# Summing the first third of a modulation on VectorE, ScalarE and GpSimd in place of TensorE

## The chip, the cores and the metric

The kernel runs as one launch on one NeuronCore of a Trainium2 chip. The metric is the device time of one execution in microseconds (us). The engines are named as in the profile: PE (TensorE), DVE (VectorE), ACT (ScalarE), POOL (GpSimd) and SP (SyncE, which here only issues transfers).

## The reference

A layer of two blocks on 256 tokens of width 1024. The first is a feed-forward network (FFN), a mixer of three attentions, and a second FFN. The second block is steered by a modulation of two conditioning vectors: `c` for the 256 tokens, and `c_ctx` for 256 context tokens.

```python
def modulation(cvec, p):
    return jnp.split(jax.nn.silu(cvec) @ p['mod_w'] + p['mod_b'], 6, axis=-1)   # mod_w: [1024, 6 * 1024]
...
    h_ctx = rmsnorm(ctx, p['norm1_pre']) * (1.0 + m_ctx[1]) + m_ctx[0]          # context states
    h = rmsnorm(x, p['norm1_pre']) * (1.0 + m_lat[1]) + m_lat[0]                # tokens
    mixed, _ = token_mixer_2(h, p, ctx_states)
    x = x + m_lat[2] * rmsnorm(mixed, p['norm1_post'])
    h2 = rmsnorm(x, p['norm2_pre']) * (1.0 + m_lat[4]) + m_lat[3]
    x = x + m_lat[5] * rmsnorm(expert_choice_moe(h2, p), p['norm2_post'])       # 16 experts
```

The first third of the modulation, 2048 of its 6144 columns, is the shift and the scale of the first norm (`m[0]`, `m[1]`). It is needed for both vectors. The other two thirds are needed for `c` alone.

## The kernel before

All arrays are fp32. A dense product is made of three: each weight block of 128 rows by 1024 columns (or a regrouping of that size, 512 KB) is loaded by SP into `wraw` (four buffers), rounded by ACT to its high part `wh` (L245), and DVE subtracts that to get the low part `wl` (L246). Both parts have two buffers (`wsp`). PE then adds up high times high (L299), high weight times low input (L301) and low weight times high input (L302). In the FFN one such weight block feeds 24 products of 128x256. The text calls this a split. A new `wh` waits until PE is done with the block two before it. Four splits make one block of 256 hidden columns; then follow a tanh on ACT (L390) and two operations of DVE on PSUM (L391, L392), and every second 128 rows of hidden columns are split in turn (`fh`, `fl`).

`modulation(side, blocks, after)` (L789) is called twice: for block 0 ahead of the first FFN's blocks (`start`, L1856), and for blocks 1 and 2 in the second FFN. For each of 8 rows of 128 and two halves it loads 512 KB of `mod_w` into `mraw`, of which there are three buffers. These 16 loads a block are issued by POOL (L827).

- Block 0: four products a row and two a half, 64 in all, with `sc[:, k, :]` (32 columns, of which two are the vectors) as the stationary operand and 512 columns of `mraw` as the moving one (L831). They add up in one PSUM bank `px`, in four groups of 32 partitions.
- Blocks 1 and 2: row 0 is scaled by ACT into `acc` (L834), row 4 is multiplied and added by DVE (L836), and each of the other rows is scaled in place by ACT (L838) and added to `acc` by POOL (L839). Four products with a column of ones (L844) then sum over the partitions.

Afterwards DVE adds the bias (L846); for block 0 four transposes (L864) and small DVE operations bring the result feature-major into `mfm` (L871, L873). The context's norm (`norm_mod_T`, L879) uses it, and with it the context's recurrence (`context_states`, L1251), whose PE work lies between the blocks of the first FFN.

The order of instructions on each engine is fixed when the program is built. A planner simulates the program and lets each engine take the earliest ready instruction, those traced first ahead of others. `modulation` is traced ahead of the FFN's blocks. On the chip each engine works through its own list in order, and waits at semaphores.

Tiles of a pool that is closed give their memory to the next pool opened on the same side. The modulation's pool `md_t`, the pool of `bias_rows` (L414), and the context's pools `cx_t` and `cx_p` follow one another on the right side.

Of the kernel before, what the change touches and what calls it, by code (L numbers as in the profile page):

```python
# [18 lines left out]
T = 256  # L19
D = 1024  # L20
# [145 lines left out]
def _body(nc, tc, ctx, A, out):  # L166
# [42 lines left out]
    def rsqrt(ss, p, n, eps, op=ALU.add, pool=None):  # L209
        """1/sqrt(ss + eps) (or of max(ss, eps)) on [p, n]; ss may come in two parts to add."""  # L210
# [25 lines left out]
    def mean_sq_halves(x_ap, junk):  # L236
        """The mean square of a row in two parts, for rsqrt."""
        ss = small.tile([128, 2], F32, name="ssq")
        for nh in range(2):
            ns = slice(nh * 512, nh * 512 + 512)  # L240
            S.activation(junk[:, ns], x_ap[:, ns], AF.Square, scale=1.0 / 32, accum_out=ss[:, nh:nh + 1])
        return ss[:, 0:1], ss[:, 1:2]
# [5 lines left out]
    def transposes(dst_fn, src, n, dense=True):  # L248
        """PE-transpose n 128-column blocks of src; dst_fn(j0, k, ps) takes each bank's worth."""
# [8 lines left out]
    # this many of 1024 columns of a weight split have their low part from Pool  # L258
    share = [0]

    def wsplit(src, a, b, pool=None, name="w", eng=None, raw=None):
        """[a * 128, b] weights (a * b <= 1024) as a list of a (high, low) pairs of [128, b]."""
# [14 lines left out]
    def proj_tok(hT, w, kc, n0, n):  # L277
        """[128 tok, n] x 2 token tiles of h @ w[:, n0:n0+n]."""
# [13 lines left out]
    def proj_feat_acc(o, parts, hT, k0, bank0):  # L292
        """Accumulates feature-major products into o(c); the first to touch a bank starts it."""
# [11 lines left out]
    def proj_feat(hT, w, n0, n, take):  # L305
        """Feature-major [128 f, 256 tok] chunks of h @ w[:, n0:n0+n], n <= 512; take(c, ps)."""
# [14 lines left out]
    def norm_T(hT, t, x, xn, gain_bc):  # L321
        """rms norm of one token tile with a gain row, transposed and split in two parts into hT."""
# [6 lines left out]
    def in_turn(normed):  # L329
        """Both token tiles' norms ahead of what follows from the first."""  # L330
# [4 lines left out]
    def wide(w, nk, lhs, spare, done):  # L335
        """[T, D] of nk * 128 rows of w; the last rows' products go token tile by token tile, and
        done(t, two banks) follows each. lhs(k) gives the two parts [128, T]."""
# [27 lines left out]
    def ffn(xs, hT, gain, wg, wu, wd, hooks, then):  # L365
        """hooks: other work to issue before (-1) or after a block of hidden columns. hT is None where
        the norm is still to be done; then(pool, scratch) gives what follows for a finished token tile."""
# [43 lines left out]
    # ---------------------------------------------------------------- attention block  # L411
    skew = dram.tile([20, 128, 384], F32, name="skew")

    def bias_rows():  # L414
        """Bias by distance for every head (masked), once per partition, for a skewed load."""
# [14 lines left out]
    def attention(xs, hT, next_gain):  # L430
        """The block on the normed input hT; returns the normed input of the next, of gain next_gain."""
        with ExitStack() as fx:
# [55 lines left out]
            def evac_later(jobs, last=None):  # L488
                """(columns, take) projections, each block's take issued after the next block's products."""
# [7 lines left out]
            # ---- projections  # L497
# [65 lines left out]
            # ---- attention  # L563
            def softmax(lg, mx):
                """exp(lg - mx) in place; returns 1/sum."""
# [123 lines left out]
            def swept(attn):  # L689
                """Both query tiles, each head's output after the next one's logits."""  # L690
# [12 lines left out]
            def gates(i, nh):  # L703
                """1 + tanh of half the gate: twice its sigmoid."""
# [23 lines left out]
            def branch(w, kc, oT, nh, gs):  # L728
                """y += sigmoid(gate) * (o @ w), a factor 2 left in."""
# [55 lines left out]
    # ---------------------------------------------------------------- modulation  # L785
# [3 lines left out]
    def modulation(side, blocks, after=None):  # L789
        """Rows of silu(c) @ mod_w + mod_b; block 0 goes feature-major to mfm, the others to mrows, with  # L790
        the gains of the norms they meet (and a half) in them. For block 0 the
        tensor engine sums, for two vectors at once; the others are of one vector only, and their sums
        over a partition are Pool's. A generator: those start on each step, and end on the next."""
# [1103 lines left out]
```

## Time and profile before

| what | value |
|---|---|
| device time, median of 3 runs | 2231.14 us (2227.08 to 2231.18) |
| span of the profiled execution, first to last instruction | 2224.2 us |
| PE busy | 1826.4 us, 82% |
| DVE, ACT, POOL busy | 887.3, 589.9, 335.4 us |

The profile records one execution; it gives that execution's span, and no device time of its own beside it. The span lies 6.9 us under the median of the runs and 2.9 us under their lowest. Busy times are shares of the whole span, so they average over stages with different limits.

### The profile page before, as it was taken

What the parts mean: (1) busy time and instruction counts of PE and PEld (TensorE: products, weight loads), DVE (VectorE), ACT (ScalarE), POOL (GpSimd) and SP (SyncE); (2) the same over time, 40 slices, a digit from 0 to 9 for tenths busy, and PEclk for the clock granted to TensorE, in tenths of its full rate; (3) what the DMA queues carried; (4) which work ended last, traced back from release to release, by engine and by line L of the source; (5) the groups of instructions that cost most, each with busy time, mean ns of one, the idle gap of its engine ahead of it and who ended that gap; (6) DMA issues with size and microseconds to landing.
All of it is one profiled execution on the core that took longest, in us unless ns stands there. A gap on an engine that the chain in (4) does not pass through costs nothing.

```text
span 2224.2 us, 28420 instructions
## 1 busy us (share of the span) xinstructions
PE 1826.4 (82%) x11441; PEld 1108.2 (50%) x11442; DVE 887.3 (40%) x1611; ACT 589.9 (27%) x954; POOL 335.4 (15%) x332
## 2 busy tenths in 40 slices
PE   7999999999988899898999876766766666667775
PEld 5888877777768877888687521111111111111111
DVE  4577855865757765777647410000000000000001
ACT  3345443544436544453314200000000000000001
POOL 2111013210325540235233200000000000000000
PEclk9999989999989999989889887677677787777667
DMA  8654545444448855424336899999999999999997
GB/s 296 222 167 134 171 131 171 136 145 121 132 143 270 280 185 182 141 81 113 115 105 220 314 409 410 410 409 406 407 407 406 407 407 410 410 411 409 406 407 302
DMA packets 237046, 600.95 MB, mean 270 GB/s; under 512 B 35384, under 2 KB 91217, under 8 KB 204146
## 3 DMA queue, kind: packets, MB, share of 16 engines
q1 hardware_dynamic: 200464, 551.89, 67.6%
q0 software_dynamic: 10496, 36.08, 4.9%
q10 hardware_dynamic: 25954, 11.16, 1.9%
q8 instruction: 90, 1.47, 0.3%
q14 instruction: 42, 0.34, 0.0%
HBM read 593.25 MB, written 9.75 MB: 271 GB/s over the span
## 4 chain that ended last, share of the span: by engine, by line
DMA 42%; PE 41%; DVE 8%; ACT 3%; issue 3%; POOL 1%; SPq 0%; ACTq 0%; DVEq 0%; POOLq 0%
DMA ring<-exp_w 39%; PE mm L302 4%; PE mm L299 3%; PE mm L288 3%; PE mm L301 3%; PE mm L287 3%; PE mm L289 3%; DVE wl L246 2%; PE mm L346 2%; PE mm L345 2%; PE mm L349 2%; PE px L1779 1%; DMA wraw<-w_in 1%; ACT wh L245 1%; PE tr L1812 1%
## 5 line engine op out<-in xcount | busy, mean ns | idle before, releaser
L1779 PE MATMUL px<-ring,xeT 128*32 128x512 f32 x2048 | 370.0, 812 | 181.9 <-DMA ring<-exp_w 181.7
L246 DVE TENSOR_TENSOR wl<-wraw,wh 128x1024 fp32r<-128x1024 f32 (+2 forms) x243 | 317.5, 1307 | 174.2 <-ACT wh L245 169.9
L245 ACT ACTIVATE wh<-wraw 128x1024 fp32r<-128x1024 f32 (+2 forms) x243 | 254.5, 1048 | 352.5 <-PE mm L301 143.5
L1779 PEld LDWEIGHTS px<-ring,xeT 128*32 128x32 f32 x2048 | 48.7, 123 | 474.6 <-DMA ring<-exp_w 440.4
L302 PE MATMUL mm<-hh,wl 128*128 128x256 f32 x912 | 266.6, 294 | 18.6 <-DVE wl L246 16.6
L299 PE MATMUL mm<-hh,wh 128*128 128x256 f32 x912 | 265.7, 292 | 2.1 <-ACT hh L245 2.1
L301 PE MATMUL mm<-hl,wh 128*128 128x256 f32 x912 | 264.1, 290 | 1.7 <-DVE hl L246 1.6
L1791 DVE SCALAR_TENSOR_TENSOR mth<-mth,px 128x512 f32<-128x512 f32 x16 | 11.0, 687 | 580.4 <-ACT mth L1790 580.4
L1812 PE MATMUL tr<-ring,hid 128*32 128x512 f32 x1024 | 166.8, 758 | 77.8 <-DMA ring<-exp_w 65.1
L302 PEld LDWEIGHTS mm<-hh,wl 128*128 128x128 f32 x912 | 178.6, 196 | 33.2 <-DVE wl L246 21.4
L299 PEld LDWEIGHTS mm<-hh,wh 128*128 128x128 f32 x912 | 179.6, 197 | 11.4 <-issue 7.6
L301 PEld LDWEIGHTS mm<-hl,wh 128*128 128x128 f32 x912 | 179.5, 197 | 6.6 <-issue 3.9
L1815 ACT ACTIVATE ye<-tr 128x512 f32<-128x512 f32 x32 | 19.1, 597 | 566.7 <-PE tr L1812 566.7
L1625 POOL TENSOR_SCALAR rsz<-ss 128x1 f32<-128x1 f32 x2 | 0.6, 302 | 952.9 <-ACT ring L1625 952.8
L288 PE MATMUL mm<-wl,hh 128*128 128x512 f32 (+2 forms) x320 | 127.9, 400 | 2.3 <-DVE wl L246 2.0
L1812 PEld LDWEIGHTS tr<-ring,hid 128*32 128x32 f32 x1024 | 26.4, 124 | 203.4 <-DMA ring<-exp_w 143.8
L289 PE MATMUL mm<-wh,hl 128*128 128x512 f32 (+2 forms) x320 | 124.6, 390 | 0.0
L287 PE MATMUL mm<-wh,hh 128*128 128x512 f32 (+2 forms) x320 | 117.7, 400 | 6.7 <-DVE wi L525 3.6
L1817 PE MATMUL mm<-ye,pgT 128*128 128x512 f32 x128 | 92.8, 865 | 24.0 <-ACT ye L1815 24.0
L1792 DVE SCALAR_TENSOR_TENSOR mth<-mth,px 128x512 f32<-128x512 f32 x16 | 11.0, 687 | 253.0 <-PE px L1779 253.0
L1790 ACT ACTIVATE mth<-px 128x512 f32<-128x512 f32 x16 | 9.5, 597 | 283.5 <-PE px L1779 283.5
L1817 PEld LDWEIGHTS mm<-ye,pgT 128*128 128x128 f32 x128 | 30.1, 260 | 88.4 <-ACT ye L1815 63.7
(756 smaller groups left out, 2792.4 us busy)
## 6 DMA issues: line engine op xcount, KB each, us to landing
ring<-exp_w SPq DMA_DIRECT2D x384, 1024.0 KB
wraw<-w_in SPq DMA_DIRECT2D x107, 512.0 KB
mraw<-mod_w POOLq DMA_DIRECT2D x48, 512.0 KB, 5.1
wraw<-ffn_w_gate SPq DMA_DIRECT2D x44, 512.0 KB
wraw<-ffn_w_up SPq DMA_DIRECT2D x44, 512.0 KB
wraw<-ffn_w_down SPq DMA_DIRECT2D x44, 512.0 KB
wraw<-w_out SPq DMA_DIRECT2D x11, 512.0 KB
skew<-bd POOLq DMA_DIRECT2D x1, 3840.0 KB, 27.7
```

Of the source, the lines that this page charges most:

```text
L245: S.activation(dst_h, src, AF.Copy)
L246: (eng or V).tensor_tensor(dst_l, src, dst_h.bitcast(F32), op=ALU.subtract)
L287: PE.matmul(ps[t], hh[:, k, sl], wh, start=(k == 0), stop=False)
L288: PE.matmul(ps[t], hh[:, k, sl], wl, start=False, stop=False)
L289: PE.matmul(ps[t], hl[:, k, sl], wh, start=False, stop=(k == kc - 1))
L299: PE.matmul(o(c), wh[:, cs], hh[:, k, :], start=(k == 0 and bank0(c)), stop=False, skip_group_check=True)
L301: PE.matmul(o(c), wh[:, cs], hl[:, k, :], start=False, stop=False, skip_group_check=True)
L302: PE.matmul(o(c), wl[:, cs], hh[:, k, :], start=False, stop=(k == KC - 1), skip_group_check=True)
L345: PE.matmul(acc[t][nh], fh[:, sl], wh[:, ns], start=(k == 0), stop=False)
L1779: PE.matmul(ps[32 * g:32 * g + 32, :], xeT[:, k, es], wt[:, 0, g * 512:(g + 1) * 512], start=(k == 0), stop=(k == KC - 1), skip_group_chec ...
L1812: PE.matmul(pe2[32 * g:32 * g + 32, :], hid[:, q, 32 * g:32 * g + 32], w2t[:, g, :], start=(q == 0), stop=(q == 3), skip_group_check=True)
L1817: PE.matmul(acc[t][nh], pgT[:, t * 128:(t + 1) * 128], ye, start=(e == 0), stop=(e == NE - 1))
```

## The change

For block 0 the 64 products go. Every `mraw` is read by two engines: DVE multiplies it by the first vector's value and adds it to `acc`, and ACT multiplies it by the second vector's value into a new tile `part` (two buffers), which POOL adds to another sum `acc2`. For row 0 DVE and ACT write the sums directly. At the end two columns of ones bring both sums into one PSUM bank by eight products. `acc`, `acc2` and `part` are new tiles in `md_t` for block 0. Blocks 1 and 2 keep their operations.

```diff
-            one = tmp.tile([128, 32], F32, name="one")
-            V.memset(one, 0.0)
-            V.memset(one[:, 0:1], 1.0)
+            one = [tmp.tile([128, 32], F32, name=f"one{v}") for v in range(1 if blocks[0] else 2)]
+            for v, o in enumerate(one):
+                V.memset(o, 0.0)
+                V.memset(o[:, v:v + 1], 1.0)
...
-                if b:
-                    acc = tmp.tile([128, 2048], F32, name="acc")
-                else:
-                    ps = psX.tile([128, 512], F32, name="px")
+                acc = tmp.tile([128, 2048], F32, name="acc")
+                if b == 0:
+                    acc2 = tmp.tile([128, 2048], F32, name="acc2")
...
                         if b == 0:
-                            for gg in range(2):
-                                g = hf * 2 + gg
-                                PE.matmul(ps[32 * g:32 * g + 32, :], sc[:, k, :], raw[:, gg * 512:gg * 512 + 512],
-                                          start=(k == 0), stop=(k == KC - 1), skip_group_check=True)
+                            if k == 0:
+                                V.tensor_scalar(acc[:, hs], raw, sc[:, k, 0:1], None, op0=ALU.mult)
+                                S.activation(acc2[:, hs], raw, AF.Copy, scale=sc[:, k, 1:2])
+                            else:
+                                V.scalar_tensor_tensor(acc[:, hs], raw, sc[:, k, 0:1], acc[:, hs], op0=ALU.mult,
+                                                       op1=ALU.add)
+                                part = tmp.tile([128, 1024], F32, name="mpart", bufs=2)
+                                S.activation(part, raw, AF.Copy, scale=sc[:, k, 1:2])
+                                G.tensor_tensor(acc2[:, hs], acc2[:, hs], part, op=ALU.add)
...
-                    ps = psX.tile([128, 512], F32, name="px")
-                    for g in range(4):
-                        PE.matmul(ps[32 * g:32 * g + 32, :], one, acc[:, g * 512:g * 512 + 512], start=True, stop=True,
-                                  skip_group_check=True)
+                ps = psX.tile([128, 512], F32, name="px")
+                sums = [acc] if b else [acc, acc2]
+                for v, a_ in enumerate(sums):
+                    for g in range(4):
+                        PE.matmul(ps[32 * g:32 * g + 32, :], one[v], a_[:, g * 512:g * 512 + 512], start=(v == 0),
+                                  stop=(v == len(sums) - 1), skip_group_check=True)
```

The rest of the diff takes out comments and docstrings.

## Rows read from the trace of the kernel before

**Rows 1.** The page: busy time of each engine, and the chain that ended last.

```profile
PE 1826.4 (82%) x11441; PEld 1108.2 (50%) x11442; DVE 887.3 (40%) x1611; ACT 589.9 (27%) x954; POOL 335.4 (15%) x332
...
DMA 42%; PE 41%; DVE 8%; ACT 3%; issue 3%; POOL 1%; SPq 0%; ACTq 0%; DVEq 0%; POOLq 0%
```

**Rows 2.** Busy time by stretch: us, PE, PEld, DVE, ACT, POOL, clock, DMA.

```profile
22.00:77.00 55.00, 55.00 (x370) 39.45 (x369) 21.67 (x22) 15.71 (x18) 7.07 (x13) 1.00 0.77 251
704.00:800.00 96.00, 87.69 (x687) 81.92 (x687) 69.62 (x53) 54.95 (x56) 59.28 (x42) 1.00 0.87 285
```

**Rows 3.** The same view, the stage of the experts.

```profile
1400.00:2224.00 824.00, 548.64 (x2717) 96.62 (x2715) 38.42 (x76) 32.36 (x62) 3.29 (x5) 0.74 1.01 401
```

**Rows 4.** The chain that ended last, from 22 to 77 us.

```profile
by line: PE px L831 28.6%; PE mm L302 24.3%; PE mm L299 24.1%; PE mm L301 23.3%
```

**Rows 5.** Groups of instructions from 22 to 77 us.

```profile
L299 PE MATMUL mm<-hh,wh 128*128 128x256 f32 x102 | 29.4, 288 | 0.0
...
L831 PE MATMUL px<-mraw,sc 128*32 128x512 f32 x64 | 16.8, 605 | 0.0
L246 DVE TENSOR_TENSOR wl<-wraw,wh 128x1024 fp32r<-128x1024 f32 x13 | 15.9, 1225 | 28.5 <-ACT wh L245 25.8 <-PE px L831 2.8
...
L827 POOL DMA_DIRECT2D mraw<-mod_w x13 | 7.1, 544 | 40.6 <-PE px L831 40.6
...
L246 DVE TENSOR_TENSOR fl<-hid,fh 128x512 fp32r<-128x512 f32 x2 | 1.4, 684 | 0.0
```

**Rows 6.** Timeline of PE: start, us, instruction.

```profile
24.09 0.28 PE L299 MATMUL mm<-hh,wh 128*128 128x256 f32 x1
24.30 1.05 PE L831 MATMUL px<-mraw,sc 128*32 128x512 f32 x4
25.29 0.39 PE L301 MATMUL mm<-hl,wh 128*128 128x256 f32 x1
25.51 0.28 PE L302 MATMUL mm<-hh,wl 128*128 128x256 f32 x1
```

**Rows 7.** Groups of instructions from 704 to 800 us.

```profile
L246 DVE TENSOR_TENSOR wl<-wraw,wh 128x1024 fp32r<-128x1024 f32 x29 | 53.1, 1831 | 23.0 <-ACT wh L245 22.9
L839 POOL TENSOR_TENSOR acc<-acc,mraw 128x1024 f32<-128x1024 f32 x19 | 49.1, 2588 | 18.3 <-ACT mraw L838 18.3
...
L838 ACT ACTIVATE mraw<-mraw,sc 128x1024 f32<-128x1024 f32 x18 | 20.5, 1145 | 6.2 <-DMA mraw<-mod_w 6.1
...
L836 DVE SCALAR_TENSOR_TENSOR acc<-mraw,sc,acc 128x1024 f32<-128x1024 f32 x4 | 6.2, 1556 | 0.0
...
L844 PE MATMUL px<-acc,one 128*32 128x512 f32 x12 | 3.2, 604 | 0.0
```

**Rows 8.** Waits of PE from 704 to 800 us: total, times, longest.

```profile
PE mm L302 <- DVE wl L246: 8.3, 11, 2.8
```

**Rows 9.** Instructions on mraw: ns min/median/max, first and last start.

```profile
L839 POOL TENSOR_TENSOR acc<-acc,mraw x24: 2348/2410/3407, 678.6 to 796.9; 128x1024 f32<-128x1024 f32 x24
...
L836 DVE SCALAR_TENSOR_TENSOR acc<-mraw,sc,acc x4: 1271/1282/2390, 704.1 to 775.3; 128x1024 f32<-128x1024 f32 x4
```

**Rows 10.** Timeline of DVE in the second modulation.

```profile
720.26 2.74 DVE L246 TENSOR_TENSOR wl<-wraw,wh 128x1024 fp32r<-128x1024 f32 x1
723.61 2.85 DVE L246 TENSOR_TENSOR wl<-wraw,wh 128x1024 fp32r<-128x1024 f32 x1 [0.61 <-ACT wh L245]
```

**Rows 11.** Timeline of POOL in the same stretch.

```profile
718.92 3.00 POOL L839 TENSOR_TENSOR acc<-acc,mraw 128x1024 f32<-128x1024 f32 x1 [0.35 <-ACT mraw L838]
...
722.96 2.41 POOL L839 TENSOR_TENSOR acc<-acc,mraw 128x1024 f32<-128x1024 f32 x1
```

**Rows 12.** Instructions on ctx, columns as in Rows 9.

```profile
L241 ACT ACTIVATE xn<-ctx x4: 612/614/630, 15.8 to 85.9; 128x512 f32<-128x512 f32 x4
...
L882 DVE TENSOR_SCALAR xn<-ctx,rsr x2: 753/754/754, 19.0 to 91.8; 128x1024 f32<-128x1024 f32 x2
```

**Rows 13.** Instructions on th, columns as in Rows 9.

```profile
L391 DVE SCALAR_TENSOR_TENSOR th<-th,mm x22: 672/678/686, 30.2 to 813.0; 128x512 f32<-128x512 f32 x22
```

## The prediction

> **What bounds the kernel now.** I read the page first. PE is busy for 82% of the span, and the chain that ended last is shared by transfers and PE [rows 1]: two stages with different limits. By stretches, the last 824 us run with the DMA engines full at 401 GB/s and PE busy two thirds of the time [rows 3]. That stage can only start later or earlier; what is gained or lost ahead of it is passed on one for one. The change lies in the first FFN, so I went there. From 22 to 77 us PE is busy for all of 55.0 us, at the full granted clock of 1.00 (2.4 GHz), while DVE is busy for 21.67, ACT for 15.71 and POOL for 7.07, all of it issuing loads [rows 2]. The chain in that stretch is PE alone, and the products that go have 28.6% of it [rows 4]. So the removal is real time. The question is whether the engines that take the work over can still feed PE.
>
> **What is removed.** The 64 products run in 16 groups of four. Around one group, the last FFN product ahead of it starts at 24.09 and the second one behind it at 25.51 [rows 6], 1.42 us for what are otherwise two steps. A step of the FFN follows from the rest: with g for a group, 55.0 us hold 16 g and 306 products, 102 on L299 [rows 5] and as many on L301 and L302, and 1.42 = g + 2 steps. That gives g = 1.18 us, a step of 0.118 us, and 24 steps = 2.83 us for a split. The products cost 16 x 1.18 = 18.9 us. Added on PE are eight sums at the end. Their shape is that of line L844, four of which are one group [rows 7]; I price them as two groups, 2.4 us. Net on PE: -16.5 us.
>
> **What is added.** For each of the 14 loads behind row 0, DVE has a multiply-add of 1.28 us, and POOL an add of 2.41 us (the medians of the same shapes) [rows 9]. Row 0 has two multiplications on DVE, for which I take the 0.75 us of a one-input operation of this size [rows 12]. ACT has 16 scalings of 1.145 us [rows 7], 18.3 us, on an engine that is idle for 39 of the 55 us: hidden, as long as they don't wait for POOL ahead of a `wh`. By busy time DVE has room too: 21.7 + 14 x 1.28 + 1.5 = 41 of 55 us. If that were all, the whole -16.5 us would come through.
>
> It isn't, because DVE and POOL stand in each other's way. The second modulation shows it with the same pairs of instructions. POOL's add from 722.96 takes 2.41 us, until 725.37; the `wl` that DVE starts at 723.61 ends at 726.46, 1.09 us behind the add, and takes 2.85 us [rows 10, 11]. The one before it starts at 720.26, and ends 1.08 us after an add that ends at 721.92 [rows 10, 11]. POOL's add from 718.92 takes 3.00 instead of 2.41 us. A `wl` is 1.225 us where POOL adds nothing [rows 5] and 1.831 us on average where it does [rows 7]; the multiply-add reaches 2.39 [rows 9]. So only one of the two works at a time, and a DVE instruction with two inputs from SBUF holds the passage for 1.08 us or more, POOL's add for some 2.4.
>
> The Trainium skill says the same in SBUF — State Buffer, section Who interferes with whom: a DVE instruction with two SBUF inputs and a GpSimd instruction that reads SBUF exclude each other for a whole instruction. It adds that a DVE instruction with at most one SBUF input, outside its fast modes, is not held up. These rows bear both out. By the rule the added work is summed over DVE and POOL together, as I do below; with ports of their own the -16.5 us would stand.
>
> DVE's first operation on PSUM in the FFN, with one input from SBUF, takes 672 to 686 ns in all of its 22 instances, POOL adding or not [rows 13]; it and its like are left out of what follows.
>
> So I sum what needs the passage. The added work: 14 x (1.28 + 2.41) + 2 x 0.75 = 53.2 us. Each split of the FFN that runs meanwhile: 1.225 us, and 0.10 us for its part of `fl` (two of 0.7 us in 13 splits [rows 5]), 1.33 us. From each DVE instruction that waited I take off 0.14 us (1.225 - 1.085), its part outside the passage. PE needs 2.83 us for a split. What decides is S, the splits that the order puts among the modulation's instructions, since they have to be worked through in that order.
>
> The trace has two paces for S. In the first FFN 306/24 = 12.75 splits go with 16 loads. From 704 to 800 us, where POOL adds, 29 `wl` go with 19 adds and 4 multiply-adds [rows 7]; the code has two scalings of row 0 for every 12 adds and 2 multiply-adds, so these are some 25 loads, 1.16 splits a load. POOL's part of the new loop, an add and a load's issue of 0.544 us [rows 5], is 2.95 us, about one split. With 1.16 for 16 loads S is 18, the value I take, as it is the pace of the same operations; 13 is the low end. The high end is 24, one and a half splits a load, for an order that spreads the adds more than any stretch shows.
>
> S = 18: the passage needs 53.2 + 18 x 1.33 - 32 x 0.14 = 72.7 us, PE 18 x 2.83 = 50.9. PE loses 21.8 us. S = 13: 53.2 + 17.3 - 3.8 = 66.7 against 36.8, 29.9 lost. S = 24: 53.2 + 31.9 - 5.3 = 79.8 against 67.9, 11.9 lost.
>
> On top comes what PE loses where the passage would just do. From 704 to 800 us the passage's need is 19 x 2.41 + 29 x 1.225 + 4 x 1.28 = 86 of 96 us, and PE still waited 8.3 us for `wl` [rows 8], 0.33 us for each of 25 loads. For 16 loads: 5.3 us.
>
> **The sum.** -16.5 + 21.8 + 5.3 = +10.6 us. On the span of 2224.2 this makes 2234.8, and on the median of the runs, 6.9 us above that span, 2241 (2241.7). Ends: -16.5 + 29.9 + 5.3 = +18.7 (2250) and -16.5 + 11.9 + 5.3 = +0.7 (2232).
>
> **What moves.** The 16 loads stay on POOL's queue, but each now stands behind an add on it and waits for two readers. A late `mraw` holds up what is behind it on DVE and ACT, a `wl` and a `wh`; from 704 to 800 ACT waited 6.1 us for such loads [rows 7]. What of that reached PE is in the 8.3 us counted above; nothing more, then. The pool `md_t` grows by 24 KB a partition (8 + 8 + 2 x 4), so by the tiles' sizes the context's input no longer lies beside it but in it. Its first norm, now at 15.8 us [rows 12], comes after the modulation; that is 2.5 us on ACT and DVE (four of 0.61 us for two tiles, half of that for one, and 0.75 us and small ones), covered by the FFN's remaining splits. Without that cover PE would wait for a load, a norm and a transpose, some 8 us.
>
> **Rivals.**
> - *The adds fall into idle time, faster.* PE loses only what it lost from 704 to 800 us, 5.3 us: -16.5 + 5.3 = -11.2, 2220. It needs 53.2 + 1.33 S - 0.14 (S + 14) to stay under 2.83 S, so S = 31 or more. It decides where the sum changes sign: the loss must fall from 27.1 to 16.5, that is at S = 25. For it speaks that the first FFN has 44 such splits, so there is room to spread; against it that the modulation is traced first and that both paces read are at most 1.16 splits a load.
> - *POOL's lag is met by PE at the end, slower still.* The eight sums and four transposes stand in PE's list where the planner believed the last adds done. If the order takes no account of the exclusion, the last adds come up to the 21.8 us late, of which the FFN's own delay covers most; three adds with a `wl` between them are 3 x 3.5 = 10 us that PE stands, and the context's norm follows with its 8 us: up to +29, 2260.
> - *No change to speak of.* S between 23 and 27: within 4.5 us of now.
>
> **How the numbers follow.** The sum's case, S from 13 to 22, has a chance of 0.56; the late end 0.12; no change 0.12; the adds in idle time 0.20. The predicted time is that of the first, 2241 us, with 2236 to 2250 as its own range. From the low end I leave out the tenth where the adds cost PE almost nothing, from the high end the worse half of the late end: 2221 to 2258. A measurement of this kernel tells about 0.2%, 4.5 us, from no change. Slower by more: 0.56 + 0.12, less 0.02 for the sums just under the bound, 0.66. Within it: 0.14. Faster by more: 0.20.
>
> **What would show it.** In the profile of the changed kernel: line L831 gone from the chain between 22 and 77 us and waits of PE for `wl` in its place, 20 us or more in total, none now; `wl` at 1.6 us or more on average while POOL adds; the modulation's last add some 70 us after its first multiply-add or later; about 18 `wl` between its first and its last add. The granted clock may fall where PE waits; at the passage's pace that is hidden. The prediction is wrong if there are 25 or more splits among the adds, if `wl` stays at 1.23 us, or if PE makes up the loss later in the first FFN, where it would have to be waiting now.

## The result, and the profile after

The changed kernel takes 2244.15 us (median of 4, 2236.98 to 2249.23) where the kernel before takes 2230.41 (median of 4): a ratio of 1.0067 with an interval of 1.0044 to 1.0091. Measured once more beside other runs of the kernel before it is 1.0082 (1.0063 to 1.0102). So it is slower by 10 to 23 us over both intervals. The profiled execution is the longest of the four, with a span of 2247.5 us.

The page of the changed kernel, where PE has 9.5 us less to do than in [rows 1] and DVE and POOL 48.7 and 38.2 more, and its chain:

```profile
PE 1816.9 (81%) x11393; PEld 1110.8 (49%) x11394; DVE 936.0 (42%) x1629; ACT 606.9 (27%) x970; POOL 373.6 (17%) x346
...
PE 41%; DMA 41%; DVE 10%; ACT 4%; issue 3%; POOL 1%; SPq 1%; ACTq 1%; DVEq 0%; POOLq 0%
```

Busy time by stretch of the changed kernel, with the columns of [rows 2]:

```profile
22.00:77.00 55.00, 40.76 (x287) 39.54 (x285) 50.92 (x31) 27.00 (x29) 34.88 (x22) 0.88 0.70 215
20.00:92.00 72.00, 55.53 (x387) 53.07 (x387) 67.21 (x40) 34.67 (x36) 44.09 (x26) 0.89 0.68 209
107.00:124.00 17.00, 4.71 (x18) 3.26 (x18) 10.93 (x30) 4.46 (x11) 7.51 (x12) 0.59 0.70 239
```

From 22 to 77 us PE was busy throughout before, at a clock of 1.00 [rows 2]; it is now busy for 40.76 us, at 0.88. From 20 to 92 us, the modulation's time, it stands for 16.5 us. A second gap lies at 107 to 124 us, with 4.7 us of work in 17 and a clock of 0.59, most of that stretch at the lower level of 1.2 GHz. The groups of instructions from 20 to 92 us:

```profile
L302 PE MATMUL mm<-hh,wl 128*128 128x256 f32 x128 | 40.3, 315 | 16.1 <-DVE wl L246 16.1
...
L838 POOL TENSOR_TENSOR acc<-acc,mpart 128x1024 f32<-128x1024 f32 x14 | 38.1, 2720 | 14.8 <-ACT mpart L837 14.7
L834 DVE SCALAR_TENSOR_TENSOR acc<-mraw,sc,acc 128x1024 f32<-128x1024 f32 x14 | 29.6, 2113 | 1.5 <-DMA mraw<-mod_w 1.5
L246 DVE TENSOR_TENSOR wl<-wraw,wh 128x1024 fp32r<-128x1024 f32 x16 | 29.2, 1832 | 3.6 <-ACT wh L245 3.6
...
L837 ACT ACTIVATE mpart<-mraw,sc 128x1024 f32<-128x1024 f32 x14 | 16.0, 1141 | 1.3 <-DMA mraw<-mod_w 1.1 <-POOL acc L838 0.2
L828 POOL DMA_DIRECT2D mraw<-mod_w x12 | 6.8, 567 | 9.9 <-DVE acc L834 9.3 <-ACT acc L832 0.6
L246 DVE TENSOR_TENSOR fl<-hid,fh 128x512 fp32r<-128x512 f32 x2 | 5.8, 2893 | 0.0
```

The `wl`, 1225 ns before [rows 5], now takes 1832; the multiply-add takes 2113 and POOL's add 2720 on average. The waits of PE from 22 to 130 us (us in total, times, longest):

```profile
PE mm L302 <- DVE wl L246: 16.1, 7, 4.3
PE tr L254 <- DVE xn L890: 11.0, 2, 6.8
PE px L424 <- DMA ctx<-ctx: 1.9, 1, 1.9
PE mm L299 <- ACT chh L245: 1.3, 1, 1.3
PE px L852 <- DVE acc L834: 0.4, 1, 0.4
```

The first gap is PE's wait for `wl`. The second has the waits for the context's norm (11.0 us) and one of 1.9 us at the bias's products (`px`, L424): the profile puts that to the context's load, which those products don't read; their own table is loaded just ahead of it on the same queue (from 103.5 us). How DVE and POOL hold one another up is seen in DVE's timeline of the changed kernel (start, us, instruction):

```profile
57.58 1.27 DVE L834 SCALAR_TENSOR_TENSOR acc<-mraw,sc,acc 128x1024 f32<-128x1024 f32 x1
58.78 2.89 DVE L246 TENSOR_TENSOR fl<-hid,fh 128x512 fp32r<-128x512 f32 x1
61.59 3.52 DVE L246 TENSOR_TENSOR wl<-wraw,wh 128x1024 fp32r<-128x1024 f32 x1
```

and in POOL's beside it:

```profile
57.67 3.45 POOL L838 TENSOR_TENSOR acc<-acc,mpart 128x1024 f32<-128x1024 f32 x1 [0.57 <-ACT mpart L837]
...
61.66 2.36 POOL L838 TENSOR_TENSOR acc<-acc,mpart 128x1024 f32<-128x1024 f32 x1
```

POOL's add at 57.67 comes 0.09 us behind DVE's multiply-add and takes 3.45 us, 1.04 over its 2.41 [rows 9]. `fl`, 0.68 us where it is alone [rows 5], starts while that add runs and takes 2.89. The next `wl` is recorded from 61.59, before `fl` has ended, the next add from 61.66; the add goes through in 2.36 us, and the `wl` takes 3.52: it ends at 65.11, 1.09 behind the end of the add at 64.02. That is the pattern of [rows 10, 11]. Held here are `fl` and `wl`; elsewhere in the passage the multiply-add is, for up to 3.50 us. All three are DVE operations with two inputs in SBUF, and "the passage" stands, as in the prediction, for what only one of the two engines has at a time.

### The profile page after: what moved, and what is told of

Read it like the earlier page. It is cut to its first block, busy times and chain, and to the rows that moved or that the text cites. A ratio compares the mean times of both kernels' runs of the same rounds, so it can differ in the third digit from the quotient of the medians.

```text
span 2247.5 us, 28386 instructions
## 1 busy us (share of the span) xinstructions
PE 1816.9 (81%) x11393; PEld 1110.8 (49%) x11394; DVE 936.0 (42%) x1629; ACT 606.9 (27%) x970; POOL 373.6 (17%) x346
## 4 chain that ended last, share of the span: by engine, by line
PE 41%; DMA 41%; DVE 10%; ACT 4%; issue 3%; POOL 1%; SPq 1%; ACTq 1%; DVEq 0%; POOLq 0%
DMA ring<-exp_w 38%; PE mm L302 4%; PE mm L301 4%; PE mm L299 4%; PE mm L288 3%; DVE wl L246 3%; PE mm L287 3%; PE mm L289 3%; PE mm L346 2%; PE mm L349 2%; PE mm L345 2%; PE px L1787 1%; ACT wh L245 1%; PE tr L1820 1%; PE mm L254 1%
## 5 line engine op out<-in xcount | busy, mean ns | idle before, releaser
L1787 PE MATMUL px<-ring,xeT 128*32 128x512 f32 x2048 | 364.3, 802 | 184.6 <-DMA ring<-exp_w 184.5
L246 DVE TENSOR_TENSOR wl<-wraw,wh 128x1024 fp32r<-128x1024 f32 (+2 forms) x243 | 329.2, 1356 | 133.3 <-ACT wh L245 128.8
L302 PE MATMUL mm<-hh,wl 128*128 128x256 f32 x912 | 268.5, 296 | 30.0 <-DVE wl L246 28.9
L302 PEld LDWEIGHTS mm<-hh,wl 128*128 128x128 f32 x912 | 180.3, 198 | 41.3 <-DVE wl L246 35.5
L1825 PEld LDWEIGHTS mm<-ye,pgT 128*128 128x128 f32 x128 | 30.1, 260 | 89.2 <-ACT ye L1823 63.7
## 6 DMA issues: line engine op xcount, KB each, us to landing
skew<-bd POOLq DMA_DIRECT2D x1, 3840.0 KB, 20.4
```

Of the source, the lines that this page charges most:

```text
L246: (eng or V).tensor_tensor(dst_l, src, dst_h.bitcast(F32), op=ALU.subtract)
L302: PE.matmul(o(c), wl[:, cs], hh[:, k, :], start=False, stop=(k == KC - 1), skip_group_check=True)
L1787: PE.matmul(ps[32 * g:32 * g + 32, :], xeT[:, k, es], wt[:, 0, g * 512:(g + 1) * 512], start=(k == 0), stop=(k == KC - 1), skip_group_chec ...
L1825: PE.matmul(acc[t][nh], pgT[:, t * 128:(t + 1) * 128], ye, start=(e == 0), stop=(e == NE - 1))
```

## The experiments

The prediction's theory is that DVE's operations with two inputs in SBUF and POOL's adds exclude one another, and that their sum sets PE's pace. The runs test it against others. The letters are those of the expectations: in the first two runs theory A has two costs, the exclusion and the context's norm, which comes late because `md_t` has grown, and theory B has the exclusion alone; from "no adds" on, A is the exclusion. Each ratio is against the kernel before on the same chip, with its 95% interval. As a marker inside the span I use the last operation of the first FFN's eleventh and last block (L392). The kernel before, instructions of that line from 95 us on (count, ns, first start = fifth block, last start = eleventh):

```profile
L392 DVE TENSOR_TENSOR hid<-th,mm x7: 668/686/690, 99.0 to 244.6; 128x512 f32<-128x512 f32 x7
```

and the changed one:

```profile
L392 DVE TENSOR_TENSOR hid<-th,mm x7: 673/689/689, 105.2 to 265.9; 128x512 f32<-128x512 f32 x7
```

It is 6.2 us late at the fifth block and 21.3 at the eleventh. Each marker is read from one profiled execution; the two kernels that were profiled twice moved by 1.8 us at the eleventh block and by up to 5.1 at the end of the second FFN. Up to the eleventh block PE has done the same products of FFN and context in the changed kernel as before, the modulation's apart. At the fifth it hasn't: the kernel before has by then done 3.2 us of work, the context's 16 transposes and the bias's products, that the changed kernel does behind it.

**Context early.** `acc`, `acc2` and `part` go to a pool on the other side, so that the context keeps the memory that it has before.

```diff
+            own = tmp if blocks[0] else fx.enter_context(tc.tile_pool(name="md_s", bufs=1))
...
-                acc = tmp.tile([128, 2048], F32, name="acc")
+                acc = own.tile([128, 2048], F32, name="acc")
...
-                    acc2 = tmp.tile([128, 2048], F32, name="acc2")
+                    acc2 = own.tile([128, 2048], F32, name="acc2")
...
-                                part = tmp.tile([128, 1024], F32, name="mpart", bufs=2)
+                                part = own.tile([128, 1024], F32, name="mpart", bufs=2)
```

> The changed kernel with acc, acc2, part and the second column of ones in a pool on the left side, so that the context's input keeps its own memory and its first norm runs early again. Theory A (two costs: DVE and POOL exclude each other during the modulation, some +6 us net at the fifth hidden block; the context's norm behind the modulation, some +16 us at the sixth): the sixth block's lateness falls from 22 us to 6, the end to between +2 and +8 us against the kernel before. Theory B (all of the loss is the exclusion, the gap of PE at 107 to 124 us would come in any case): lateness at the sixth block stays near 20 us, the end at +12 to +16.

Measured: 1.0054 (1.0034 to 1.0075), 2241.5 us. The waits of PE from 22 to 130 us in it:

```profile
PE mm L302 <- DVE wl L246: 14.3, 8, 4.5
PE tr L254 <- DVE xn L891: 6.4, 1, 6.4
```

The wait for `wl` is much as in the changed kernel; that for the context's norm is 6.4 us in place of 11.0. The instructions on `ctx` in it (first and last start) say why some is left:

```profile
L241 ACT ACTIVATE xn<-ctx x4: 614/626/632, 15.8 to 102.2; 128x512 f32<-128x512 f32 x4
```

The first of the two tiles' norms is early again, the second comes behind the modulation as before, and the modulation is still late. The sixth block (from DVE's timeline) is 10.2 us late in place of 22.0, where A had 6 and B 20; the eleventh is 9.6 late instead of 21.3, so the early context is worth 11.7 us there. At the end the kernel is 8 to 17 us behind by the interval, over A's 2 to 8 and around B's 12 to 16, and the intervals of 1.0054, 1.0067 and 1.0082 overlap. So both costs are there, but A's sizes weren't right: the context has a part of the loss, and most is left.

**Context late, without the change.** The kernel before, with 24 KB more in `md_t`.

```diff
+                    pads = [tmp.tile([128, 2048], F32, name=f"pad{i}") for i in range(3)]
+                    for p_ in pads:
+                        V.memset(p_[:, 0:1], 0.0)
...
+                for p_ in pads:
+                    V.tensor_copy(p_[:, 0:1], m[:, 0:1])
```

> The kernel before, its 64 products kept, with 24 KB a partition added to the modulation's pool, so that only the context's input comes late. Theory A: no change up to the fifth hidden block, then a gap of PE of some 16 us before the sixth, of which 4 to 9 us are given back later: +5 to +14 us at the end. Theory B: within 3 us of the kernel before.

Measured: 1.0003 (0.9983 to 1.0023). The first norm of the context is as late as planned, in this kernel's instructions on `ctx`

```profile
L241 ACT ACTIVATE xn<-ctx x4: 615/617/632, 78.3 to 87.7; 128x512 f32<-128x512 f32 x4
```

(first start 78.3 us instead of 15.8 [rows 12]), and the eleventh block still comes 4.1 us earlier than before (240.6). The 5 to 14 us that theory A had here didn't come: by itself the late context costs nothing in the kernel with its products. It costs where the adds make the modulation late too.

**No adds.** As "context early", without POOL's 14 adds.

```diff
-                                G.tensor_tensor(acc2[:, hs], acc2[:, hs], part, op=ALU.add)
```

> As e1_ctx_early, with POOL's 14 additions to acc2 left out, so the second vector's sum lacks rows 1 to 7. DVE and ACT keep all their new instructions. Theory A (the exclusion makes the loss): wl at 1.23 us and multiply-adds at 1.28 us throughout, PE without waits for wl, and the removal of the products shows whole: -14 to -17 us at the fifth block, -8 to -17 at the end. Rival C (the new instructions on DVE and ACT hold up wl and wh in their lists, additions or not): the fifth block as late as in e1_ctx_early, +3 to +6 us.

Measured: 0.9922 (0.9898 to 0.9946), 2210.29 us, 31.2 us under "context early". Groups of instructions in it from 20 to 100 us:

```profile
L246 DVE TENSOR_TENSOR wl<-wraw,wh 128x1024 fp32r<-128x1024 f32 x22 | 26.9, 1222 | 7.6 <-ACT wh L245 7.6
L835 DVE SCALAR_TENSOR_TENSOR acc<-mraw,sc,acc 128x1024 f32<-128x1024 f32 x14 | 18.0, 1283 | 2.4 <-DMA mraw<-mod_w 1.9 <-DVE acc L835 0.2
```

and the same groups in "context early":

```profile
L835 DVE SCALAR_TENSOR_TENSOR acc<-mraw,sc,acc 128x1024 f32<-128x1024 f32 x14 | 35.3, 2522 | 1.2 <-DMA mraw<-mod_w 1.2
L246 DVE TENSOR_TENSOR wl<-wraw,wh 128x1024 fp32r<-128x1024 f32 x18 | 30.7, 1703 | 1.0 <-ACT wh L245 1.0
```

DVE has the same operations of the modulation to do in both; without the adds they take 1222 and 1283 ns each, and all of it fits; PE waits 1.6 us for `wl` from 22 to 95 us. Against the kernel before the 16.5 us that this saves (2226.77 - 2210.29) match the -16.5 of the prediction's removal (at the eleventh block 12.7 of them stand, 231.9 against 244.6). The interval at the end is 12 to 23 us. That DVE's or ACT's own added work is the price is refuted: the loss of "context early" comes with the adds. (The order on the engines is made anew for each kernel, so these runs differ in order too; the times of 1222 and 1283 ns for one operation don't hang on it.)

**POOL writes and doesn't read.** As "context early", with each add replaced by two fills of `part`.

```diff
-                                G.tensor_tensor(acc2[:, hs], acc2[:, hs], part, op=ALU.add)
+                                for q_ in range(2):
+                                    G.memset(part, 0.0)
```

> As e1_ctx_early, with each of POOL's 14 additions replaced by two memsets of part, so POOL is busy about as often but reads nothing (the second vector's sum lacks rows 1 to 7). Theory A in the form that two-input DVE instructions exclude POOL's reads: wl at 1.23 us, multiply-add at 1.28, 12 to 17 us faster than the kernel before, as e3_no_adds. Rival E (any POOL instruction excludes them): wl at 1.5 us or more, within 8 us of the kernel before.

Measured: 0.9957 (0.9937 to 0.9977). POOL's fills in it (ns min/median/max, first and last start)

```profile
L840 POOL MEMSET mpart<- x28: 952/957/987, 24.2 to 67.3; 128x1024 f32 x28
```

and DVE's groups from 20 to 100 us:

```profile
L246 DVE TENSOR_TENSOR wl<-wraw,wh 128x1024 fp32r<-128x1024 f32 x22 | 26.7, 1219 | 5.9 <-ACT wh L245 5.9
L835 DVE SCALAR_TENSOR_TENSOR acc<-mraw,sc,acc 128x1024 f32<-128x1024 f32 x14 | 17.9, 1281 | 3.0 <-DMA mraw<-mod_w 3.0
```

POOL is busy for 28 x 0.96 = 27 us with 512 KB at a time, between 24 and 68 us, and DVE's operations keep their 1219 and 1281 ns. So it is what POOL reads that holds DVE up, not that POOL works or writes (no run has a POOL operation that reads one input). The Trainium skill has this distinction in SBUF — State Buffer, section Who interferes with whom: a DVE instruction with two SBUF inputs contends with a GpSimd instruction that reads SBUF, and not with one that only writes it. This trace agrees, at 1219 ns beside 28 fills against 1703 beside the 14 adds of "context early". The gain of 11.3 us by the medians (2215.04 against 2226.3; 5 to 14 by the interval) is less than I had expected. At the eleventh block this kernel is 2.0 us behind "no adds" (233.97 against 231.94), and PE has 2.9 us of waits ahead of it that "no adds" hasn't, for the context's norm and at the bias's products. At the end the two gains, 5 to 14 and 12 to 23 us, overlap, so whether more lies between them isn't known.

**Adds in halves.** As "context early", each add in two of 512 columns.

```diff
-                                G.tensor_tensor(acc2[:, hs], acc2[:, hs], part, op=ALU.add)
+                                for q in range(2):
+                                    hq = slice(hf * 1024 + q * 512, hf * 1024 + q * 512 + 512)
+                                    G.tensor_tensor(acc2[:, hq], acc2[:, hq], part[:, q * 512:q * 512 + 512], op=ALU.add)
```

> As e1_ctx_early, with each of POOL's additions in two of 512 columns, some 1.25 us each. Theory A as the prediction summed it (the passage's total decides, not the length of one hold): DVE can get in between, but POOL's total stays, so 1.003 to 1.008 of the kernel before, as e1_ctx_early. Rival F (the length of a hold decides, since a wl that meets a whole addition comes too late): half the loss, 0.997 to 1.001.

Measured: 1.0067 (1.0042 to 1.0093). Groups of DVE in it from 20 to 100 us

```profile
L246 DVE TENSOR_TENSOR wl<-wraw,wh 128x1024 fp32r<-128x1024 f32 x19 | 34.4, 1815 | 2.6 <-ACT wh L245 2.6
L835 DVE SCALAR_TENSOR_TENSOR acc<-mraw,sc,acc 128x1024 f32<-128x1024 f32 x14 | 28.6, 2042 | 1.1 <-DMA mraw<-mod_w 1.1
```

and of POOL:

```profile
L841 POOL TENSOR_TENSOR acc<-acc,mpart 128x512 f32<-128x512 f32 x28 | 54.6, 1969 | 7.0 <-ACT mpart L838 6.9
```

Shorter holds don't help, against rival F. An add of half the size takes 1.28 us at the least of 28 and 1.97 on average. The passage is asked for as long as before (28 x 1.28 = 35.8 us against 14 x 2.41 = 33.7), and PE waits 12.4 us for `wl`, against 14.3 with whole adds.

**Both vectors on DVE.** As "context early", but DVE multiplies and adds the second vector too; POOL only issues loads.

```diff
-                                S.activation(part, raw, AF.Copy, scale=sc[:, k, 1:2])
-                                G.tensor_tensor(acc2[:, hs], acc2[:, hs], part, op=ALU.add)
+                                V.scalar_tensor_tensor(acc2[:, hs], raw, sc[:, k, 1:2], acc2[:, hs], op0=ALU.mult,
+                                                       op1=ALU.add)
```

> As e1_ctx_early, with the second vector's products and sum on DVE as well (28 multiply-adds and 4 multiplications), none on ACT and POOL. Theory A: every instruction at its own time (wl 1.23, multiply-add 1.28); DVE's list of 28 x 1.28 + 4 x 0.75 + 15 splits at 1.67 = 64 us against 42 us of PE for 15 splits, 22 us lost against 16.5 removed: +3 to +8 us. If the order puts 20 splits in: 72 against 57, -1. Rival C as for e3_no_adds would make it worse than e1_ctx_early, above +8.

Measured: 1.0027 (1.0011 to 1.0043). Its groups on DVE from 20 to 100 us (after the bar: busy us, mean ns, idle us before them):

```profile
L246 DVE TENSOR_TENSOR wl<-wraw,wh 128x1024 fp32r<-128x1024 f32 x19 | 23.0, 1216 | 0.7 <-ACT wh L245 0.7
L837 DVE SCALAR_TENSOR_TENSOR acc<-mraw,sc,acc 128x1024 f32<-128x1024 f32 x14 | 17.9, 1277 | 0.0
L835 DVE SCALAR_TENSOR_TENSOR acc<-mraw,sc,acc 128x1024 f32<-128x1024 f32 x14 | 17.9, 1277 | 0.0
```

Nothing is held up (1216 and 1277 ns), and DVE is full: 0.7 us idle ahead of 19 `wl`. PE waits 9.0 us for `wl` from 22 to 95 us. The second vector's multiply-adds on DVE are 14 x 1.28 = 17.9 us where POOL's adds hold the passage for 14 x 2.41 = 33.7. That is 15.8 us less, and the kernel is 7.9 us faster than "context early" by the medians and 9.7 at the eleventh block (244.5 against 254.2). Two engines that exclude one another do no more than one, and here less, as the add is dearer on POOL.

**Half of the columns on DVE.** The first 1024 of the 2048 columns stay with 32 products on PE; of the others DVE sums both vectors, and POOL and ACT add nothing.

```diff
+                            if hf == 0:
+                                for g in range(2):
+                                    PE.matmul(ps[32 * g:32 * g + 32, :], sc[:, k, :], raw[:, g * 512:g * 512 + 512],
+                                              start=(k == 0), stop=(k == KC - 1), skip_group_check=True)
+                            else:
+                                for v in range(2):
...
+                                        V.scalar_tensor_tensor(sums[v], raw, sc[:, k, v:v + 1], sums[v], op0=ALU.mult,
+                                                               op1=ALU.add)
```

> The first 1024 of the 2048 columns stay with 32 products on PE; the other 1024 are summed on DVE for both vectors (14 multiply-adds, 2 multiplications) and brought in by four products of ones. POOL adds nothing. Theory A (14 multiply-adds on DVE cost PE nothing where POOL does not add, as in e3_no_adds): 8 groups of four removed, one added, -8.2 us; -5 to -9 us. Rival C (DVE's list is too full): -2 to +3 us.

Measured: 0.9991 (0.9976 to 1.0007). A stretch of it, with the columns of [rows 2]:

```profile
22.00:95.00 73.00, 73.00 (x551) 62.76 (x550) 59.26 (x84) 29.18 (x36) 13.77 (x23) 1.00 0.78 257
```

PE is busy for 73.00 of 73 us, at the full clock. The eleventh block ends 8.0 us earlier than before (236.6) and the last `hid` of the second FFN 10.4 earlier (807.7 against 818.1). The 8.2 us computed for 32 products less four sums stand there, and are gone at the end.

> The kernel of e7_half once more. Its context's states came 9.5 us earlier than in the kernel before, its time was 0.9991 [0.9976, 1.0007]. If the 8.2 us computed for it come through to the end, the ratio is 0.9955 to 0.9975; if they are given back behind the first FFN, 0.9985 to 1.0005.

Measured: 0.9992 (0.9974 to 1.001). The same, in another execution: 6.3 us ahead at the eleventh block, 5.3 at the end of the second FFN, none at the end: they are given back. I have no version that beats the kernel before.

**Adds spread out.** As "context early", with one buffer for `mraw` in place of three, so that more splits lie among the 16 loads (some 30 by plan). As the modulation then ends late, the blocks of the FFN at which the context's steps are traced move from 3 and 4 to 9 and 10.

```diff
-HOOK0 = 3
-HOOK1 = 4
+HOOK0 = 9
+HOOK1 = 10
...
-                        raw = tmp.tile([128, 1024], F32, name="mraw", bufs=3)
+                        raw = tmp.tile([128, 1024], F32, name="mraw", bufs=1 if b == 0 else 3)
```

> As e1_ctx_early, with one mraw buffer in place of three, so that a load waits for the one before it, and the context's two steps after the tenth and eleventh block in place of the fourth and fifth (HOOK0 9, HOOK1 10). Some 30 splits lie among the 16 loads in place of 15. Theory A (DVE and POOL exclude each other; the splits among the additions decide): 93 - 6 = 87 us of the passage against 85 of PE, 2 lost, 5 more for meetings, 16.5 removed: 7 to 11 us under e6_hooks_late. Rival D (each addition costs PE some 2 us wherever it stands, as it meets a wl or a multiply-add anyway): 10 to 15 us over e6_hooks_late.

The kernel before with the same late context, for comparison (the two HOOK lines alone):

> The kernel before with the context's two steps after the tenth and eleventh block (HOOK0 9, HOOK1 10): the reference for e5_spread. The context's recurrence then fills fewer gaps in the first FFN and more in the attention: -5 to +10 us against the kernel before.

Measured: 1.0236 (1.0213 to 1.0259) with the adds spread, 1.0231 (1.0211 to 1.0251) for the comparison. The context's steps are 52 us dearer in the later place by themselves, where I had expected -5 to +10. Between the two kernels there is no difference at the end: neither the 7 to 11 us under the comparison that A had, nor the 10 to 15 over it of rival D. Line L392 with the adds spread (first FFN, from 90 us on; the last start is the eleventh block)

```profile
L392 DVE TENSOR_TENSOR hid<-th,mm x6: 673/682/689, 97.8 to 162.6; 128x512 f32<-128x512 f32 x6
```

and in the comparison:

```profile
L392 DVE TENSOR_TENSOR hid<-th,mm x7: 682/687/689, 99.7 to 179.3; 128x512 f32<-128x512 f32 x7
```

The eleventh block is 16.7 us earlier, as much as the removal forecast. But that isn't the removal alone: by this marker the comparison has done the context's 16 transposes, the bias's products and the end of the modulation, which the spread kernel has still to do. And the adds don't fit. PE's waits in the spread kernel from 22 to 130 us, with ten of the adds:

```profile
PE mm L302 <- DVE wl L246: 11.6, 10, 2.6
```

Up to the eleventh block it is 13.3 us, near the 14.3 of "context early". Yet there is room in the sum: 38 `wl` lie between the first multiply-add and the last, more than the 31 splits that the prediction's first rival asks for. Its formula gives 51.7 + 38 x 1.33 - 52 x 0.14 = 95 us for the passage and 107.5 for PE, and from 33 to 161 us DVE idles for 28 us of 128. Most adds meet the multiply-add of their own load, which takes 3.45 us in nine of the 14 cases, and the `wl` behind that comes late. So room in the sum is not enough: the meetings cost 0.8 us a load here, where the prediction had 0.33.

Behind the marker the lead is lost. A stretch of the first of the two kernels, just behind its last add (from 161.8 us):

```profile
165.00:200.00 35.00, 27.27 (x179) 24.18 (x176) 23.46 (x55) 9.04 (x13) 6.17 (x10) 0.76 0.56 190
```

PE stands for 7.7 of 35 us, at a clock of 0.76, where it is full in the comparison (35.00 of 35): the bias's products and the context's second norm (its last start on ACT is 169.7 us) follow a modulation that now ends as late as the FFN. When the context's states are written this kernel is 6.2 us behind the comparison (421.7 against 415.5).

**The changed kernel again**, beside these:

> The changed kernel once more, beside the other runs, for the size of its loss and for what its late context norm adds over e1_ctx_early (1.0054 of the kernel before). If the 12.7 us by which its context's states came later than e1_ctx_early's stay to the end: 1.0100 to 1.0125. If they are given back behind: 1.0045 to 1.0080.

Measured: 1.0082 (1.0063 to 1.0102), the second measurement of the section above, just over the range for "given back"; the eleventh block at 264.1 us, 19.5 late.

## Why the prediction was right, and where it wasn't

The direction held, and so did the size: 2241 us were forecast, 10.6 over the span of before plus 6.9; 2244.15 and 2243.85 were measured. The likeliest case, with its own range of 2236 to 2250, is the one that came.

**The removal.** -16.5 us net. "No adds" has the removal with all else that DVE and ACT took over: 16.5 us under the kernel before at the end, 12.7 at the eleventh block. So it is near, and the exact agreement at the end is luck, as one part was priced too low. The trace has two instructions for each of these fp32 products of the code: the 64 that the text ahead counts are 32 in the code, two to a group, and the eight sums are 16 instructions (L852). They run in three stretches of 1.05, 1.07 and 1.05 us, three groups where the prediction has two. That makes 13 groups of 1.18 us, -15.3.

**The passage.** Taken: S = 18, 21.8 us lost, and 5.3 for meetings, 27.1 together. In DVE's timeline of the changed kernel 15 `wl` start between the first multiply-add (20.4 us) and the last (89.2); with the context early it is 16. The formula at S = 15, without the 1.5 us of row 0, which lies ahead, gives 51.7 + 15 x 1.33 - 29 x 0.14 = 67.6 us of passage; measured are 70.1, from 20.4 to 90.5. The prediction's sum takes the 0.14 us off all DVE instructions, though it names only those that waited; in the timeline 12 of the 29 take over 1.5 us, and with 0.14 off these alone the sum is 70.0. For PE, 128 products on L302 are 16 splits, which with one group of sums take 16 x 2.83 + 1.2 = 46.5 of the 72 us from 20 to 92: 25.5 lost, 16.5 of them as waits and the rest as slower steps at a clock of 0.89. At the fifth block it is 6.2 + 15.3 + 3.2 (the work that moved behind the marker) = 24.7. So the mechanism was right and the term some 2 us too large: S was three too high, which alone would make the loss too small (26.6 at 15 against 21.8), and of the 5.3 us for meetings little is left to see, as the passage is nearly full from end to end. Luck is in that: where it isn't full, in "adds spread out", the meetings cost more than was put down for them.

**What moves.** This is the step that failed: the late norm of the context was put at nothing, "covered by the FFN's remaining splits". Between the fifth and the eleventh block the kernel loses another 15.1 us (21.3 - 6.2); without the 3.2 us of work that only moved it is 11.9. The instructions on `ctx` in the changed kernel (ns min/median/max, first and last start):

```profile
L241 ACT ACTIVATE xn<-ctx x4: 614/623/632, 107.7 to 114.7; 128x512 f32<-128x512 f32 x4
...
L1270 ACTq DMA_DIRECT2D ctx<-ctx x2: 444/468/493, 103.8 to 104.3; - x2
L890 DVE TENSOR_SCALAR xn<-ctx,rsr x2: 752/752/753, 111.3 to 119.9; 128x1024 f32<-128x1024 f32 x2
```

The load is issued at 103.8 us, behind the modulation's end on ACT's queue, and the norm starts at 107.7, in place of 15.8 [rows 12]. PE's timeline there:

```profile
104.91 0.28 PE L302 MATMUL mm<-hh,wl 128*128 128x256 f32 x1
107.08 0.80 PE L424 MATMUL px<-onehot,table 32*20 32x384 f32 x2 [1.90 <-DMA ctx<-ctx]
112.07 1.97 PE L254 MATMUL tr<-ident,xn 128*128 128x128 f32 x8 [4.19 <-DVE xn L890]
120.83 1.94 PE L254 MATMUL tr<-ident,xn 128*128 128x128 f32 x8 [6.79 <-DVE xn L890]
```

Behind 105 us PE's list has the bias's products and the context's transposes and no split of the FFN; it stands 1.90, 4.19 and 6.79 us. That order suits a modulation that ends on time. The cover that I named is there in "context late" (no cost), where the adds don't run late, and not here. The four cases at the eleventh block, against the kernel before: context late alone, with the products still on PE, -4.1; no adds, context early -12.7; adds, context early +9.6; adds and context late +21.3. The two delays are no sum: the second costs 11.7 with the first and nothing without (as far as the kernel with its products shows; no run has a late context with neither products nor adds). The price without cover, "some 8 us", was too low too. I had it in the late rival, with a chance of 0.12 and beside sums of PE that stand; the sums didn't stand (0.4 us for `px` in the waits above), the norm did.

**What stood behind.** The errors have opposite signs: some 2 us too much in the passage, 1.2 too much taken off for the removal, 11.9 too little for the context; +21.3 at the eleventh block, where the sum has +10.6. The second FFN's end (L391 on `th`, 827.6 against 813.0 [rows 13]) is 14.6 us late, the end by the medians of the two measurements 13.7 and 19.0. The two traces end 23.3 us apart, as the profiled execution of the changed kernel is the longest of its four. The prediction passes every gain and loss on to the end one for one. That holds for the last stage: from the experts' first product (1262.2 us before, 1283.5 changed) to the end every kernel here takes 961.5 to 965.4 us. It doesn't hold for the second block's mixer ahead of it: "half of the columns" goes from 10.4 us early at the second FFN's end to 3.0 at the experts' first product, and "both vectors on DVE" from 9.1 early to 6.5 late. PE's order there differs between the kernels, as the order is made anew when the program is built. No run settles by which wait. The adds by themselves ("context early" less "no adds") are 22.3 us at the eleventh block and 31.2 at the end, around the 27.1 forecast. So the agreement at the end, +10.6 against +13.7 and +19.0, is partly luck; what the runs bear out is the sign, the mechanism and the size of the passage.

**The tells.** `wl` at 1.6 us or more: 1.83. Last add some 70 us behind the first multiply-add: 64.5 to its start (20.4 to 84.9), 67.8 to its end. `wl` among the adds, about 18: 15. Waits for `wl` of 20 us or more: 16.1, and 12.9 for the context's norm and the bias's products, which I hadn't named there. The clock fell to 0.89 from 20 to 92 us; that it is hidden there, as predicted, is argued from DVE, which idles for only 4.8 of 72 us.

**The rivals.** That the adds fall into idle time was refuted for this order, and "adds spread out" doesn't bear it out in another one either: with 38 splits among the adds PE still waits 13.3 us for `wl`, where the rival has 5.3. That nothing changes was refuted by both intervals.

## What to carry to other kernels

Count DVE's operations with two SBUF inputs and POOL's operations that read SBUF as work of one engine: work moved from a full PE to this pair costs about what their sum has over PE's time in the same stretch, which here is 70 us against 43. A sum below PE's time doesn't make it free: with the adds spread it was 95 against 107.5, and PE waited 13.3 us. Ask of each tile that grows whose memory it takes, and whether the engine that waits for it has work listed behind the wait; a delay that costs nothing alone can cost its full length behind another one. And a gain in one stage is real only at the end: 10.4 and 5.3 us that stood at 818 us in the two runs of "half of the columns" were gone at the last instruction.

## What the runs showed of the hardware

- A fill on POOL (128x1024 fp32, 957 ns) holds no DVE operation up, an add of the same size on POOL does: `wl` 1219 ns beside 28 fills, 1703 to 1832 beside 14 adds.
- Even an operation half the size is held for all of an add: `fl` (128x512) took 2.89 us where it takes 0.68, and `wl` up to 3.52, nearly three times its 1.22. Who goes first can't be read from the recorded starts, which overlap on one engine.
- Cutting POOL's adds into smaller pieces brought nothing: an add of 512 columns took 1.97 us on average, 1.28 at the least, so 3.9 us for the pair where one add of 1024 columns took 2.74 in "context early".
- Room in the sum of both engines didn't keep them apart: with DVE idle for 28 of 128 us, nine of 14 multiply-adds still met an add and took 3.45 us in place of 1.28.
- Where PE stood in waits of 4 to 7 us, its granted clock was 0.59 over 17 us, near the lower level of 1.2 GHz, and eight transposes took 1.97 us where they take 1.04 in "context late", at a clock of 1.00.
